# Down projection of a ConvFFN: sample products in six visits, raw weight tiles in a ring of nine, first operands of the second group formed early

## The chip, the core and the metric

The kernel runs on one core of a Trainium2 chip. The metric is the device time of one execution in microseconds, taken as the median of several runs. The engines are PE (TensorE, matrix products; PEld is its weight load), DVE (VectorE), ACT (ScalarE), POOL (GpSimd) and SP (SyncE, which here only issues DMAs). Each engine works through its own instructions in a fixed order. Arrays are fp32; data lies in SBUF with 128 partitions, and PE writes into eight banks of PSUM.

## The reference

One inference step of a one-layer streaming encoder: a token mixer, then a feed-forward part, for 1024 prompt tokens and 32 sample tokens. Only the feed-forward part's last product matters here:

```python
def conv_ffn(xn, buf, w_up, conv_w, conv_b, w_down):
    up = xn @ w_up
    up, buf = causal_dwconv(up, buf, conv_w, conv_b)
    gate, val = jnp.split(up, 2, axis=-1)
    return (jax.nn.gelu(gate, approximate=True) * val) @ w_down, buf
...
x = x + rms_norm(h, g_ffn_post[l])
```

`h = gelu(gate) * val` has 2816 channels, `w_down` is 2816 x 1024.

## The kernel before, in words

The up projection computes h for the prompt in 22 tiles of 128 channels x 1024 tokens (`up_finish`), which go to the DRAM array `h_d`, one DMA each on SP's queue. For the 32 sample tokens it leaves h in SBUF, as `smp_h`.

The down projection (`down_all`) computes the prompt's product with seven products of quarter size, after Strassen: P2, P1, P4, P6, P5, P7, P3, in that order. Each (`run`) loops over p = 0..10 (`NP` = 11), and in each p over four blocks of 128 tokens. An fp32 product is made of three: each operand is split into a high half (a cast on ACT, line 94) and a low half (a subtraction on DVE, line 97), and `mm3` multiplies high by high, high by low and low by high (lines 88, 89, 90). So one p is 12 products of 128 x 512. The operands of step p of product P1 are called P1h (from the tile `ht`, loaded from `h_d`) and P1w (from a raw weight tile, named `wrP` in the profile). ht0 to ht10 belong to P1, ht11 to ht21 to P2. I write "P2 4" for the raw weight tile that P2's p = 4 takes; P2 uses weights 11 to 21, P1 uses 0 to 10, and the other products use sums of weights that were made earlier in DRAM (`ws_d`).

The split operands lie in rings: four tiles for h ("hop"), seven for weights ("op"). The raw weight tiles lie in a ring of six: two in the pool `praw[0]`, four in `ph`. A raw tile of P2 and P1 is read twice: by the split, and by the sample tokens' product.

That product is `sample_products`: the 32 sample tokens times the same raw weights, in plain fp32, for all 22 weight tiles. Four small products, of two weight tiles with two halves each, run side by side in four column groups of PE, 32 columns wide. The profile records two passes for each product (L1618, tile `s`). They are done in visits, after p = 1, 3, 5, 7, 9 and 10 of P2 (into the bank s1) and of P1 (into s2). A raw tile is free for the next load once its visit has read it.

At the end of P2, ACT copies s1 to `keep` (line 1710) and P2's four banks W to `ca` (line 1712). P1 goes into four banks x (`X`), which take the slots of the ring "xw"; s1 takes one of these slots too. Then DVE adds s2 to `keep` and the banks X to `ca`, and P4 begins.

The order of instructions on each engine is set by a planner, which runs a model of the times over the program, with the program's order as priority. `tc.issue_after(ins)` binds it: the instructions of the block stand behind `ins` on ins's engine. Waits on data and on free tiles are added by the planner. `down_raw` loads a raw tile, `load_h` a tile of h; both issue on SP, and in `load_h` the issue stands behind the last raw load (`behind["SP"]`). `rows_of` holds what is done beside each p of P2 (k = 1) and P1 (k = 0): visits and loads. P2's first loads come from `freed`, ahead of the up projection's end (`EARLY` = 3). The row `gp` (the gain of the last norm, broadcast to 128 partitions) is loaded at the start of `down_all`, and ACT turns the sign of half of it.

Of the kernel before, what the change touches and what calls it, by code (L numbers as in the profile page):

```python
# [8 lines left out]
F32 = mybir.dt.float32  # L9
# [3 lines left out]
AF = mybir.ActivationFunctionType  # L13
ALU = mybir.AluOpType
# [4 lines left out]
SEQ = 1024  # L19
# [3 lines left out]
NF = DFF // 128  # L23
# [55 lines left out]
def body(ctx: ExitStack, tc: tile.TileContext, a: dict):  # L79
    nc = tc.nc  # L80
    act, dve, pool, pe, sp = nc.scalar, nc.vector, nc.gpsimd, nc.tensor, nc.sync
# [5 lines left out]
    def mm3(ps, lh, rh, first, last, **kw):  # L87
        pe.matmul(ps, lh[0], rh[0], start=first, stop=False, **kw)  # L88
        pe.matmul(ps, lh[0], rh[1], start=False, stop=False, **kw)  # L89
        return pe.matmul(ps, lh[1], rh[0], start=False, stop=last, **kw)  # L90

    def split(hi, lo, src, eng=None, heng=None):
        if heng is None:
            act.copy(hi, src)
        else:
            heng.tensor_copy(hi, src)
        (eng or pool).tensor_tensor(lo, src, hi.bitcast(F32), op=ALU.subtract)  # L97

    def tanh(out, in_, scale):
        return act.activation(out, in_, AF.Tanh, scale=scale)  # L100
# [4 lines left out]
    psb = ctx.enter_context(tc.tile_pool(name="psb", bufs=3, space=PSUM, reuse_waits="tile"))  # L105
# [19 lines left out]
    h_d = dr.tile([NF, 128, SEQ], F32, name="h_d")  # L125
# [115 lines left out]
    cols_of, dcs_of, behind = {}, {}, {}  # L241
# [969 lines left out]
    upper, jks, kept, pgs = [], [], {}, ExitStack()  # L1211
# [205 lines left out]
    def up_finish(py, f, uu):  # L1417

        ys = []
        for i, j in enumerate((f, NF + f)):  # L1420
            u = uu[i][:, 2:]
            y = py.tile([128, SEQ], F32, tag="y", name=f"y{j}", bufs=3)
            behind["POOL"] = pool.tensor_copy(fhalo[:, j, :], u[:, SEQ - 2:SEQ])  # L1423
            act.activation(y, u, AF.Identity, scale=fconv[:, j, 2:3], bias=fconv[:, j, 3:4])  # L1424
            for s in range(2):
                dve.scalar_tensor_tensor(y, uu[i][:, s:s + SEQ], fconv[:, j, s:s + 1], y, op0=ALU.mult, op1=ALU.add)  # L1426
            ys.append(y)
        act.activation(ys[0], ys[0], AF.Gelu_apprx_tanh)
        kept["gated"] = dve.tensor_tensor(ys[0], ys[0], ys[1], op=ALU.mult)
        sp.dma_start(h_d[f], ys[0])  # L1430

    def up_samples():

# [106 lines left out]
    praw, ph, EARLY = [], [], 3  # L1540

    NP = NF // 2
# [19 lines left out]
            sorted((2 * i + 3 * t, t, i) for i in range((NP + 1) // 2) for t in range(8))]  # L1562

    wraws = {}

    def down_raw(kind, p):

        key = (kind, p if kind in ("P1", "P2") else p // 2)
        if key in wraws:
            return  # L1570
        own = len(wraws) % 6 < 2
        r = (praw[0] if own else ph[0]).tile([128, 2, 512], F32, tag="raw", name=f"wr{kind}_{p}", bufs=2 if own else 4)
        if kind in ("P1", "P2"):
            f = p + NP * (kind == "P2")
            behind["SP"] = sp.dma_start(r.rearrange("p j n -> p (j n)"), a["w_dn"][f])
        else:
            n = min(2, NP - p)
            src = a["w_dn"][NP + p:NP + p + n, :, 512:].rearrange("f p n -> p f n") if kind == "P3" else \
                ws_d[{"P5": 0, "P7": 1, "P6": 2, "P4": 3}[kind]][:, p:p + n, :]
            behind["SP"] = sp.dma_start(r[:, :n, :], src)  # L1580
        wraws[key] = r

    hts = {}

    def load_h(pool_, f):
        hts[f] = pool_.tile([128, SEQ], F32, name=f"ht{f}")
        with tc.issue_after(behind["SP"].ins):
            sp.dma_start(hts[f], h_d[f])

    def ablk(i, k, p):  # L1590
        h = hts[p + NP * k]
        return h[:, 512 * i:512 * i + 512]

    ASRC = dict(P1=(0, 0), P2=(0, 1), P4=(1, 1), P6=(0, 0), P5=(1, 1), P7=(1, 0), P3=(0, 1))

    def halves_of(src, name, pool_, tag, bufs):
        t = pool_.tile([128, 2, 512], F32R, tag=tag, name=name, bufs=bufs)
        split(t[:, 0], t[:, 1], src, dve)
        return t[:, 0], t[:, 1]

    def down_operands(ph, kind, p, early=False):
        down_raw(kind, p)
        h = halves_of(ablk(*ASRC[kind], p), f"{kind}h{p}", ph, "hop", 4)
        wp = (ph, "hop", 4) if early else (praw[1], "op", 7)
        if kind in ("P1", "P2"):
            r = wraws[kind, p]
            w = halves_of(r[:, 0], f"{kind}w{p}", *wp)
        else:
            w = halves_of(wraws[kind, p // 2][:, p % 2], f"{kind}w{p}", *wp)
        return h, w  # L1610

    def sample_products(ps, k, p):

        with tc.issue_after(behind["PE"].ins):
            for q in range(p - p % 2, p + 1):
                for j in range(2):
                    r = 64 * (q % 2) + DEC * j
                    pe.matmul(ps[r:r + DEC], smp_h[:, q + NP * k, :], wraws["P2" if k else "P1", q][:, j],  # L1618
                              start=q < 2, stop=q >= NP - 2)

    def down_all(ph, pc, begun, late):

        CA = pc.tile([128, 4, 2, 512], F32, name="ca")
        CB = pc.tile([128, 4, 2, 512], F32, name="cb")
        gp = pc.tile([128, 1024], F32, name="gp")
        sp.dma_start(gp, a["grows"][1:2, :].broadcast_to([128, 1024]))
        act.activation(gp[:, 512:], gp[:, 512:], AF.Copy, scale=-1.0)
        ssp = late.enter_context(tc.tile_pool(name="p11", bufs=1, side="right", reuse_waits="tile"))

        def w_banks(name):  # L1630
            return [psf.tile([128, 512], F32, tag="sx", name=f"{name}0", bufs=1)] + \
                [psb.tile([128, 512], F32, tag="big", name=f"{name}{i}", bufs=3) for i in range(1, 4)]

        def run(kind, banks, first, last, each=None, n_end=0):
            end = []
            for p in range(NP):
                ops = begun.pop((kind, p), None) or down_operands(ph, kind, p)
                if p >= NP - n_end:
                    end.append((p, ops))
                    continue  # L1640
                h, w = ops
                for i in range(4):
                    c = slice(128 * i, 128 * i + 128)
                    behind["PE"] = mm3(banks[i], (h[0][:, c], h[1][:, c]), w, first and p == 0, last and p == NP - 1,
                                       skip_group_check=True)
                if each:
                    each(p, w)
            return end
# [41 lines left out]
        def scratch(u):  # L1690
            return pc.tile([128, 4], F32, tag="fss", name=f"gss{u}", bufs=9)

        def rows_of(k, bank):

            def each(p, w):
                if p % 2 or p == NP - 1:
                    sample_products(bank, k, p)
                if k:
                    for f in (NP + EARLY + p, p - NP + 6):
                        if 0 <= f < NF and f not in hts:  # L1700
                            load_h(ph if f >= NP else ssp, f)
                elif p + 6 < NP:
                    load_h(ssp, p + 6)
            return each

        s1 = psf.tile([128, 512], F32, tag="xw", name="s1", bufs=4)
        W = w_banks("q2")
        run("P2", W, True, True, rows_of(1, s1))
        keep = pc.tile([128, 512], F32, name="keep")
        act.copy(keep, s1)  # L1710
        for i in range(4):
            act.copy(CA[:, i, 0], W[i])

        X = [psf.tile([128, 512], F32, tag="xw", name=f"x{i}", bufs=4) for i in range(4)]
        s2 = psb.tile([128, 512], F32, tag="big", name="s2", bufs=3)
        run("P1", X, True, False, rows_of(0, s2))
        dve.tensor_tensor(keep, keep, s2, op=ALU.add)
        quarter = pc.tile([DEC, 3, 512], F32, name="quarter")
        for b in range(3):
            sp.dma_start(quarter[:, b], keep[DEC * (b + 1):DEC * (b + 2)])  # L1720
# [3 lines left out]
        W = w_banks("q4")  # L1724
# [9 lines left out]
        W = w_banks("q5")  # L1734
# [35 lines left out]
        W = w_banks("q3")  # L1770
# [10 lines left out]
        def each(p, w):  # L1781
            if p < 4:
                upper_half(p)
# [76 lines left out]
    p4s, p5s, p6s, p7s, p8s, p9s, pxs, phs, late = (ExitStack() for _ in range(9))  # L1860
# [3 lines left out]
    psf = p4s.enter_context(tc.tile_pool(name="psf", bufs=1, space=PSUM, reuse_waits="tile"))  # L1864
# [5 lines left out]
    own = {"c1": pt.tile([128, 256], F32, name="c1_00")}  # L1870
# [7 lines left out]
    X = col_operands(px, q0, 0, parts="B")  # L1878
# [49 lines left out]
    begun = {}  # L1928

    def freed():  # L1930
        pxs.close()
        ph.append(phs.enter_context(tc.tile_pool(name="ph", bufs=1, side="left", reuse_waits="tile")))
        for p in range(EARLY):
            down_raw("P2", p)
            load_h(ph[0], NP + p)
        down_raw("P2", EARLY)
# [166 lines left out]
```

## Time and profile before

| what | value |
|---|---|
| median of 3 runs | 1350.47 us (1350.0 to 1354.46) |
| the profiled execution | 1351.36 us, its span 1349.6 us |
| granted TensorE clock, mean | 0.988 |
| PE busy | 1301.8 us (96%) |
| DVE, ACT, POOL busy | 1009.9, 700.2, 281.7 us |
| P2's first product to P1's last | 1110.5 to 1189.2 us |
| L1618, 88 passes | 1120.8 to 1190.2 us |
| P4 and P6 | 1190.1 to 1250.2 us |

A line of the order in time gives the start in us from the span's start, the length, the engine, the line of the kernel, the operation, out<-in, the shape and the number of merged instructions; in brackets stands the idle time of the engine ahead of it and what ended it. The chain of work gives start, length, engine, tile and line. A line on one tile's instructions gives the shortest, median and longest in ns, and when the first and the last start.

### The profile page before, as it was taken

Reading aid. Unit: us, or ns where it says so; the run is one execution under the profiler, and the core shown is the slowest. Engines: PE = TensorE matmul, PEld = TensorE weight load, DVE = VectorE, ACT = ScalarE, POOL = GpSimd, SP = SyncE. Lnnn points to the kernel's source line nnn. Section 1 sums busy time; section 2 is a strip of 40 time slices with the busy share of each in tenths; the row PEclk is TensorE's granted clock in tenths of the full one; section 3 lists DMA queues with packets and bytes.
Section 4 is the critical chain, followed back from the end, with each engine's and each line's share of the span. In section 5 each row is a group of like instructions: output and inputs, shape, how many; then the busy total and the mean of one; then the engine's idle time right before and its main releaser. Section 6 shows DMA issues by size and latency. Waiting matters only on the chain.

```text
span 1349.6 us, 25577 instructions
## 1 busy us (share of the span) xinstructions
PE 1301.8 (96%) x9896; PEld 1097.7 (81%) x9896; DVE 1009.9 (75%) x1761; ACT 700.2 (52%) x1298; POOL 281.7 (21%) x399
## 2 busy tenths in 40 slices
PE   6999999998999999999999999999999999999997
PEld 6999899998888987767877777778888886678885
DVE  5795649778698778876898676778888875499566
ACT  5555556555575555535754444444555454454552
POOL 4531403136022254313100010110111000010005
PEclk9999999999998999989999999999999999999998
DMA  8699878886789964543627988864674349644435
GB/s 339 233 350 362 279 245 256 281 282 219 270 254 313 326 200 134 183 146 104 192 82 237 312 225 282 217 185 134 155 168 137 99 158 356 254 162 141 144 106 124
DMA packets 134784, 291.73 MB, mean 216 GB/s; under 512 B 29015, under 2 KB 63991, under 8 KB 132535
## 3 DMA queue, kind: packets, MB, share of 16 engines
q1 hardware_dynamic: 121031, 267.03, 58.4%
q0 software_dynamic: 9120, 18.62, 7.8%
q10 hardware_dynamic: 4512, 4.46, 1.0%
q8 instruction: 77, 1.26, 0.4%
q14 instruction: 44, 0.36, 0.1%
HBM read 229.38 MB, written 85.78 MB: 234 GB/s over the span
## 4 chain that ended last, share of the span: by engine, by line
PE 64%; DVE 8%; ACT 2%; issue 1%; POOL 1%; DMA 1%; DVEq 0%; POOLq 0%; SPq 0%; ACTq 0%
PE pux_None L88 4%; PE pux_None L89 4%; PE pux_None L90 4%; PE q L88 3%; PE puw_None L88 3%; PE puw_None L89 3%; PE puw_None L90 3%; PE q L89 3%; PE q L90 3%; PE x L88 2%; PE x L89 2%; PE x L90 2%; PE zp L90 2%; PE zp L88 2%; PE zp L89 2%; PE us L1457 2%
## 5 line engine op out<-in xcount | busy, mean ns | idle before, releaser
L1426 DVE SCALAR_TENSOR_TENSOR y<-uu,fconv_sb,y 128x1024 f32<-128x1024 f32 x88 | 112.8, 1282 | 22.9 <-ACT y L1424 21.8
L1423 POOL COPY fhalo<-uu 128x2 f32<-128x2 f32 x44 | 17.1, 388 | 388.8 <-DVE uu L1341 388.8
L88 PE MATMUL pv<-wt_0h,xh 128*128 128x256 f32 (+1 forms) x192 | 55.9, 291 | 5.5 <-DVE xl L321 1.6
L90 PE MATMUL zp<-woh,cl 128*128 128x512 f32 (+1 forms) x144 | 57.3, 398 | 1.4 <-DVE cl L1093 1.4
L1424 ACT ACTIVATE y<-uu,fconv_sb 128x1024 f32<-128x1024 f32 x44 | 54.8, 1245 | 6.8 <-DVE uu L1341 5.9
L88 PE MATMUL zp<-woh,ch 128*128 128x512 f32 (+1 forms) x144 | 56.9, 405 | 1.0 <-ACT ch L1092 0.8
L89 PE MATMUL zp<-wol,ch 128*128 128x512 f32 (+1 forms) x144 | 57.4, 399 | 0.3 <-DVE wol L97 0.3
L90 PE MATMUL pv<-wt_1h,xl 128*128 128x256 f32 (+1 forms) x192 | 54.9, 286 | 0.0
L88 PE MATMUL pv<-wt_1h,xh 128*128 128x256 f32 (+1 forms) x192 | 54.5, 284 | 0.0
L90 PE MATMUL pv<-wt_0h,xl 128*128 128x256 f32 (+1 forms) x192 | 54.4, 283 | 0.0
L89 PE MATMUL pv<-wt_0l,xh 128*128 128x256 f32 (+1 forms) x192 | 54.2, 282 | 0.0
L89 PE MATMUL pv<-wt_1l,xh 128*128 128x256 f32 (+1 forms) x192 | 54.2, 282 | 0.0
L1673 POOL TENSOR_TENSOR gss<-gss 128x1 f32<-128x1 f32 (+1 forms) x9 | 8.6, 952 | 185.1 <-ACT gjk L1666 185.1
L208 POOL TENSOR_SCALAR hrs<-hss 128x5 f32<-128x5 f32 (+3 forms) x27 | 10.1, 376 | 174.5 <-DVE hss L1002 171.9
L88 PEld LDWEIGHTS pv<-wt_0h,xh 128*128 128x128 f32 x192 | 35.9, 187 | 7.6 <-DVE xl L321 2.2
L818 DVE COPY_PREDICATED P<-masks_sb,sc 128x352 f32<-128x352 int32 (+3 forms) x53 | 37.8, 713 | 5.0 <-PE sc L731 4.4
L209 POOL TENSOR_TENSOR hrs<-hrs,mhalf 128x5 f32<-128x5 f32 (+3 forms) x27 | 37.2, 1376 | 2.2
L88 PEld LDWEIGHTS pv<-wt_1h,xh 128*128 128x128 f32 x192 | 35.9, 187 | 0.7 <-issue 0.6
L1002 DVE TENSOR_REDUCE hss<-sq 128x5 f32<-128x320 f32 (+3 forms) x27 | 13.6, 502 | 30.4 <-ACT sq L1001 30.4
L90 PEld LDWEIGHTS pv<-wt_1h,xl 128*128 128x128 f32 x192 | 35.9, 187 | 0.3
L90 PEld LDWEIGHTS pv<-wt_0h,xl 128*128 128x128 f32 x192 | 35.9, 187 | 0.2
L89 PEld LDWEIGHTS pv<-wt_0l,xh 128*128 128x128 f32 x192 | 35.9, 187 | 0.1
(1898 smaller groups left out, 4652.3 us busy)
## 6 DMA issues: line engine op xcount, KB each, us to landing
wus<-in_w_us SPq DMA_DIRECT2D x16, 1024.0 KB, 6.3
wrP<-in_w_dn SPq DMA_DIRECT2D x27, 512.0 KB, 3.9
h_d<-y SPq DMA_DIRECT2D x22, 512.0 KB, 4.4
ht<-h_d SPq DMA_DIRECT2D x22, 512.0 KB, 7.1
wt_0r<-in_w_tok SPq DMA_DIRECT2D x21, 512.0 KB, 5.6
wt_1r<-in_w_tok SPq DMA_DIRECT2D x21, 512.0 KB, 6.6
ws_d<-in_w_dn POOLq DMA_DIRECT2D x20, 512.0 KB, 6.6
wrP<-ws_d SPq DMA_DIRECT2D x20, 512.0 KB, 3.9
```

The lines of the kernel that those rows point to most:

```text
L88: pe.matmul(ps, lh[0], rh[0], start=first, stop=False, **kw)
L89: pe.matmul(ps, lh[0], rh[1], start=False, stop=False, **kw)
L90: return pe.matmul(ps, lh[1], rh[0], start=False, stop=last, **kw)
L208: pool.tensor_scalar(out, ss, 1.0 / width, eps, op0=ALU.mult, op1=ALU.add)
L209: pool.tensor_tensor(out, out, mhalf[:n, :cols], op=ALU.pow)
L818: dve.copy_predicated(dst, mk.broadcast_to([n, 11, *mk.shape[2:]]), src)
L1002: dve.tensor_reduce(ss[:n, h0:h0 + nh], sq3, axis=mybir.AxisListType.X, op=ALU.add)
L1423: behind["POOL"] = pool.tensor_copy(fhalo[:, j, :], u[:, SEQ - 2:SEQ])
L1424: act.activation(y, u, AF.Identity, scale=fconv[:, j, 2:3], bias=fconv[:, j, 3:4])
L1426: dve.scalar_tensor_tensor(y, uu[i][:, s:s + SEQ], fconv[:, j, s:s + 1], y, op0=ALU.mult, op1=ALU.add)
L1457: pe.matmul(ps[DEC * q:DEC * q + DEC], smp_x[:, k, :], ring[i % 3][:, q, :], start=k == 0, stop=k == 7)
L1673: pool.tensor_tensor(ss[:n, 0:1], ss[:n, 2:3], ss[:n, 3:4], op=ALU.add)
```

## The change

- `sample_products` takes a list of weight tiles, and is called after p = 3 (tiles 0 to 3), p = 7 (4 to 7) and p = 9 (8 to 10, with the raw tile of p = 10 asked for first) of P2 and of P1: six visits in all. The bank s2 is taken at the first visit of P1, s1 at that of P2.
- The ring of raw tiles has nine slots for P2 and P1: two in `praw[0]`, five in `ph`, two in `ssp`, the pool of ht0 to ht10; seven for the later products. Their loads are bound to stand in order.
- `load_h` now counts as the last load on SP, so that the next one stands behind it. P2's loads of raw tiles 4 to 10 and of ht17 to ht20 are asked for after p = 3, then P1's raw tiles 0 and 1 and ht21. P1's raw tiles 2 and 3 follow at p = 7, then ht0; ht1 and ht2 at p = 8, ht3 and ht4 at p = 9, and ht5 at p = 10. `gp` is loaded after p = 9, and its sign turned at P1's p = 1.
- P1's operands of p = 0 and 1 are formed at the end of P2. In P1, the cast of each h stands on ACT behind the cast of the weights before it. `keep` stands behind the cast of P1's second h, and the copies to `ca` behind `keep`, asked for at P1's p = 1.
- The last store to `h_d` is issued by POOL.

The core of the diff:

```diff
-        sp.dma_start(h_d[f], ys[0])
+        (pool if f == NF - 1 else sp).dma_start(h_d[f], ys[0])
...
+    VISITS_D = {3: range(4), 7: range(4, 8), NP - 2: range(8, NP)}
...
-        own = len(wraws) % 6 < 2
-        r = (praw[0] if own else ph[0]).tile([128, 2, 512], F32, tag="raw", name=f"wr{kind}_{p}", bufs=2 if own else 4)
+        n = len(wraws) % (9 if kind in ("P1", "P2") else 7)
+        pool_, bufs = (praw[0], 2) if n < 2 else (ph[0], 5) if n < 7 else (praw[2], 2)
+        r = pool_.tile([128, 2, 512], F32, tag="raw", name=f"wr{kind}_{p}", bufs=bufs)
...
-            behind["SP"] = sp.dma_start(r.rearrange("p j n -> p (j n)"), a["w_dn"][f])
+            with ExitStack() as order:
+                if wraws:
+                    order.enter_context(tc.issue_after(behind["raw"].ins))
+                behind["raw"] = behind["SP"] = sp.dma_start(r.rearrange("p j n -> p (j n)"), a["w_dn"][f])
...
+        if f not in hts:
+            place_h(pool_, f)
         with tc.issue_after(behind["SP"].ins):
-            sp.dma_start(hts[f], h_d[f])
+            behind["SP"] = sp.dma_start(hts[f], h_d[f])
...
-        h = halves_of(ablk(*ASRC[kind], p), f"{kind}h{p}", ph, "hop", 4)
+        late = tc.issue_after(kept["w"].ins) if kind == "P1" and p else ExitStack()
+        with late:
+            h = halves_of(ablk(*ASRC[kind], p), f"{kind}h{p}", ph, "hop", 4)
+            kept["h"] = kept["w"]
...
-                if p % 2 or p == NP - 1:
-                    sample_products(bank, k, p)
+                if p == 1:
+                    first()
+                if p in VISITS_D:
+                    if p == NP - 2:
+                        down_raw("P2" if k else "P1", p + 1)
+                    banks.append(banks[0] if banks else bank())
+                    sample_products(banks[0], k, VISITS_D[p])
+                if k and p == 3:
+                    for q in range(p + 1, NP):
+                        down_raw("P2", q)
+                        if q < 8:
+                            load_h(ph, NP + EARLY - 1 + q)
                 if k:
-                    for f in (NP + EARLY + p, p - NP + 6):
-                        if 0 <= f < NF and f not in hts:
-                            load_h(ph if f >= NP else ssp, f)
-                elif p + 6 < NP:
-                    load_h(ssp, p + 6)
+                    if p < 3:
+                        load_h(ph, NP + EARLY + p)
+                    if p == 3:
+                        for q in range(2):
+                            down_raw("P1", q)
+                        load_h(ph, NF - 1)
+                    if p == 7:
+                        for q in range(2, 4):
+                            down_raw("P1", q)
+                    if p == NP - 1:
+                        for q in range(2):
+                            begun["P1", q] = down_operands(ph, "P1", q)
+                    for f in {7: (0,), 8: (1, 2), 9: (3, 4), 10: (5,)}.get(p, ()):
+                        load_h(ssp, f)
+                else:
+                    if p + 4 < NP:
+                        down_raw("P1", p + 4)
+                    if p + 6 < NP:
+                        load_h(ssp, p + 6)
...
+        def leave_q2():
+            with tc.issue_after(kept["keep"].ins):
+                for i in range(4):
+                    act.copy(CA[:, i, 0], W[i])
...
-        act.copy(keep, s1)
-        for i in range(4):
-            act.copy(CA[:, i, 0], W[i])
+        with tc.issue_after(kept["h"].ins):
+            kept["keep"] = act.copy(keep, srow[0])
...
-        run("P1", X, True, False, rows_of(0, s2))
-        dve.tensor_tensor(keep, keep, s2, op=ALU.add)
+        run("P1", X, True, False, rows_of(0, lambda: sample_bank(psb, "big", "s2", 3), leave_q2))
+        dve.tensor_tensor(keep, keep, srow[1], op=ALU.add)
```

More of the change, by code (lines that the diff above doesn't have):

```diff
@@ L92, in split @@
     def split(hi, lo, src, eng=None, heng=None):
[L93 to L96, printed above, removed]
+        ins = act.copy(hi, src) if heng is None else heng.tensor_copy(hi, src)
         (eng or pool).tensor_tensor(lo, src, hi.bitcast(F32), op=ALU.subtract)
+        return ins
     def tanh(out, in_, scale):
@@ L1583, in body, with place_h @@
     hts = {}
+    def place_h(pool_, f):
+        hts[f] = pool_.tile([128, SEQ], F32, name=f"ht{f}")
+    loaded = set()
     def load_h(pool_, f):
-        hts[f] = pool_.tile([128, SEQ], F32, name=f"ht{f}")
+        if f in loaded:
+            return
+        loaded.add(f)
+        if f not in hts:
+            place_h(pool_, f)
         with tc.issue_after(behind["SP"].ins):
-            sp.dma_start(hts[f], h_d[f])
+            behind["SP"] = sp.dma_start(hts[f], h_d[f])
     def ablk(i, k, p):
@@ L1597, in halves_of @@
         t = pool_.tile([128, 2, 512], F32R, tag=tag, name=name, bufs=bufs)
-        split(t[:, 0], t[:, 1], src, dve)
+        kept["w"] = split(t[:, 0], t[:, 1], src, dve)
         return t[:, 0], t[:, 1]
@@ L1610, in down_operands, with sample_products @@
         return h, w
-    def sample_products(ps, k, p):
+    def sample_products(ps, k, qs):
         with tc.issue_after(behind["PE"].ins):
-            for q in range(p - p % 2, p + 1):
+            for q in qs:
                 for j in range(2):
@@ L1625, in down_all @@
         gp = pc.tile([128, 1024], F32, name="gp")
-        sp.dma_start(gp, a["grows"][1:2, :].broadcast_to([128, 1024]))
-        act.activation(gp[:, 512:], gp[:, 512:], AF.Copy, scale=-1.0)
         ssp = late.enter_context(tc.tile_pool(name="p11", bufs=1, side="right", reuse_waits="tile"))
+        praw.append(ssp)
+        for f in range(4):
+            place_h(ssp, f)
         def w_banks(name):
@@ L1691, in scratch, with rows_of @@
             return pc.tile([128, 4], F32, tag="fss", name=f"gss{u}", bufs=9)
-        def rows_of(k, bank):
+        def rows_of(k, bank, first=lambda: None):
+            banks = []
             def each(p, w):
-                if p % 2 or p == NP - 1:
-                    sample_products(bank, k, p)
-                if k:
-                    for f in (NP + EARLY + p, p - NP + 6):
-                        if 0 <= f < NF and f not in hts:
-                            load_h(ph if f >= NP else ssp, f)
-                elif p + 6 < NP:
-                    load_h(ssp, p + 6)
-            return each
@@ L1706, in down_all @@
-        s1 = psf.tile([128, 512], F32, tag="xw", name="s1", bufs=4)
+                if p == 1:
[10 more added lines that the diff above has]
+                            load_h(ph, NP + EARLY - 1 + q)
@@ new lines, in each, with sample_bank @@
+                if k and p == 9:
+                    with tc.issue_after(behind["SP"].ins):
+                        sp.dma_start(gp, a["grows"][1:2, :].broadcast_to([128, 1024]))
+                if not k and p == 1:
+                    act.activation(gp[:, 512:], gp[:, 512:], AF.Copy, scale=-1.0)
+            return each
+        def sample_bank(pool_, tag, name, bufs):
+            srow.append(pool_.tile([128, 512], F32, tag=tag, name=name, bufs=bufs))
+            return srow[-1]
+        def leave_q2():
+            with tc.issue_after(kept["keep"].ins):
+                for i in range(4):
+                    act.copy(CA[:, i, 0], W[i])
@@ L1707, in down_all @@
+        srow = []
         W = w_banks("q2")
-        run("P2", W, True, True, rows_of(1, s1))
+        run("P2", W, True, True, rows_of(1, lambda: sample_bank(psf, "xw", "s1", 4)))
         keep = pc.tile([128, 512], F32, name="keep")
-        act.copy(keep, s1)
-        for i in range(4):
-            act.copy(CA[:, i, 0], W[i])
+        with tc.issue_after(kept["h"].ins):
+            kept["keep"] = act.copy(keep, srow[0])
         X = [psf.tile([128, 512], F32, tag="xw", name=f"x{i}", bufs=4) for i in range(4)]
-        s2 = psb.tile([128, 512], F32, tag="big", name="s2", bufs=3)
```

## The prediction, made before the changed kernel ran

> **What bounds the kernel now.** I read the page's busy times first, then the stretches of the down projection, then the chain of work, then each engine in order of time around the two places that the diff touches.
>
> ```profile
> PE 1301.8 (96%) x9896; PEld 1097.7 (81%) x9896; DVE 1009.9 (75%) x1761; ACT 700.2 (52%) x1298; POOL 281.7 (21%) x399
> 1121.00:1150.00 29.00, 29.00 (x143) 19.59 (x136) 14.72 (x22) 10.78 (x19) 0.00 (x0) 1.00 0.97 346
> 1150.00:1156.00 6.00, 4.13 (x16) 1.90 (x15) 1.71 (x3) 4.71 (x9) 0.00 (x0) 1.00 1.03 420
> 1156.00:1190.00 34.00, 34.00 (x164) 22.56 (x162) 20.01 (x33) 13.50 (x25) 0.00 (x0) 1.00 0.62 220
> 1220.00:1240.00 20.00, 20.00 (x90) 16.57 (x89) 20.00 (x35) 10.99 (x22) 1.63 (x2) 1.00 0.41 112
> ```
>
> The columns of a stretch are its length, then busy time of PE, PEld, DVE, ACT, POOL, the granted clock, DMA share and GB/s. TensorE bounds the kernel, and in the groups P2 and P1 (1110 to 1190 us) it is busy throughout except for 1.87 us in 1150 to 1156, where P2 hands over to P1. So the change can win there by taking PE work out or by closing that gap, and nowhere else in these 80 us. The last row warns: in P6 DVE is as full as PE.
>
> **The six visits.** Before, `sample_products` runs after p = 1, 3, 5, 7, 9, 10 of each group, 12 visits; after, after p = 3, 7, 9, 6 visits. The products are the same.
>
> ```profile
> 1138.84 1.00 PE s L1618 x8
> 1145.51 1.00 PE s L1618 x8
> 1158.56 1.00 PE s L1618 x8
> 1189.18 0.98 PE s L1618 x4
> 1203.08 0.91 PE q L90 x4
> 1205.80 0.91 PE q L90 x4
> 1132.11 1.06 PE L1618 MATMUL s<-wrP,smp_h 128*32 128x512 f32 x8
> L1618 PE MATMUL s<-wrP,smp_h x88: 592/605/617, 1120.8 to 1189.6; 128*32 128x512 f32 x88
> ```
>
> Without visits a p of 12 products takes 1205.80 - 1203.08 = 2.72 us, 0.227 each. From visit to visit there are 1145.51 - 1138.84 = 6.67 us, and 24 products are 5.44, so a visit costs 1.23. Its eight passes go four at a time, in two rounds: first start to last end 1.06, one pass 0.605, so a round takes 0.455 and two take 0.91. The other 0.32 is entry and exit. The visit with four passes takes 0.98, as long as one with eight, so rounds are paid, not passes. Rounds stay at 12 per group (4 + 4 + 4 for 2 x 6, since p = 10 alone also takes two). Six entries go: 6 x 0.32 = 1.9 us. Bounds: 0, if the 0.32 goes with each pair of rounds, to 1.9. A loss is excluded as no pass is added. I take 1.9, because the four-pass row says that the extra does not follow the amount of work in a visit.
>
> The Trainium skill, "TensorEngine Tiling (Array Packing)", Key Properties, says that changing the tiling mode drains the TensorE, while tiles within one mode run independently. The visits change from 128 to 32 columns and back, so by it 12 of 24 changes go. By the contrary reading, a cost of each 32-column round, nothing would go and the sum would be 2.4 in place of 4.3. The rows agree with the drain as far as one visit shows; no row has four rounds in a visit.
>
> **The hand-over from P2 to P1.**
>
> ```profile
> 1151.73 0.96 PE L90 MATMUL x<-P1w,P1h 128*128 128x512 f32 x3
> 1153.34 0.50 PE L88 MATMUL x<-P1w,P1h 128*128 128x512 f32 x1 [0.64 <-ACT keep L1710]
> 1155.53 1.20 PE L88 MATMUL x<-P1w,P1h 128*128 128x512 f32 x4 [1.23 <-ACT P1w L94]
> 1150.23 2.05 ACT L1712 COPY ca<-q 128x512 f32<-128x512 f32 x4 [4.03 <-PE q L90]
> 1152.14 0.65 ACT L94 CAST P1h<-ht 128x512 fp32r<-128x512 f32 x1
> 1152.66 0.62 ACT L1710 COPY keep<-s 128x512 f32<-128x512 f32 x1
> 1154.34 0.62 ACT L94 CAST P1h<-ht 128x512 fp32r<-128x512 f32 x1 [1.05 <-PE x L90]
> 1154.86 1.14 ACT L94 CAST P1w<-wrP 128x512 fp32r<-128x512 f32 x2
> ```
>
> ACT had stood idle 4.03 us before the four `ca` copies. `keep` frees the bank of the fourth x product and waits behind them, and the weights of P1's p = 1 wait behind an h cast that itself waits for PE. Price: 1158.56 - 1145.51 = 13.05 us between two visits, less two visits (2.46) and 36 products (12 of P2, 24 of P1: 8.16), leaves 2.43. After the change both operands of p = 0 and 1 are formed ahead, `keep` follows P1h1's cast, the last P2 visit stands at p = 9, one p (2.72 us) before the end, and the `ca` copies (2.05 on ACT) come at p = 1, needed by nobody before s2's bank at p = 3. I take the whole 2.43; bounds 0 to 2.43, and below zero only through late tiles.
>
> **Tiles on SP's queue.** This is where a cost can come in. SP issues in order; load_h is now chained behind the last load of either kind.
>
> ```profile
> 1125.54 1.22 DVE L1429 TENSOR_TENSOR y<-y,y 128x1024 f32<-128x1024 f32 x1
> 1127.43 0.38 SPq L1430 DMA_DIRECT2D h_d<-y  x1
> 1127.87 0.42 SPq L1626 DMA_DIRECT2D gp<-in_grows  x1
> 1135.89 5.25 SPq L1588 DMA_DIRECT2D ht<-h_d  x8
> 1137.10 0.63 ACT L1627 ACTIVATE gp<-gp 128x512 f32<-128x512 f32 x1 [1.91 <-DMA gp<-in_grows]
> 1144.02 0.62 ACT L94 CAST P2h<-ht 128x512 fp32r<-128x512 f32 x1 [3.11 <-DMA ht<-h_d]
> DMA to landing us min/median/max: 3.5/3.9/10.0
> L1559 POOL DMA_DIRECT2D ws_d<-in_w_dn x24: 855/1145/1814, 732.9 to 1044.3; - x24
> DMA to landing us min/median/max: 4.3/6.6/9.9
> ```
>
> The first landing row is that of the raw tiles (wrP), the second that of POOL's transfers to ws_d. Before, the last gated tile is ready at 1126.76; its store is issued at 1127.43, ht21 is issued 8.5 us later, once the store has landed, and P2h10 is cast 3.11 us late, though still ahead of PE. POOL issues the store after: it costs POOL 0.9 to 1.8 us (idle there) and lands 4.3 to 9.9 us after issue, so 1131 to 1137, and ht21 is no later than now. Nine raw slots let P2 4 to 8 start without a visit's release; P2 9 and 10 and P1 0 and 1 wait for the visit at p = 3. PE reaches it one visit earlier than now, 1125.51 - 1.23 = 1124.3, and leaves it at 1126.4.
>
> New is a wait: P1 2 and 3 take the slots of P2 4 and 5, freed inside the visit at p = 7 (1126.4 + 4 x 2.72 = 1137.3, tiles free about 1138.4), and ht0 to ht5 and gp are queued behind them. At 420 GB/s (stretch 1150 to 1156) 512 KB take 1.25 us. P1 2 lands about 1138.4 + 3.9 = 1142.3, or 1143 with the issues between, P1 3 1144.3, ht0 1145.5, ht1 1146.8. PE leaves P2 at 1137.3 + 2.1 + 5.44 + 2.1 + 2.72 = 1149.7. P1h0 needs ht0 plus cast and subtraction (0.62 + 0.69): 1146.8, ready 2.9 us ahead; P1h1 1148.1, needed 1152.4; `keep` after its cast, 1148. So it fits, with 2.9 us of cover; every us that ht0 is later than that costs one.
>
> gp's load moves from 1127.87 to about 1142 and its scaling on ACT (0.63) to P1's p = 1. With the 9.2 us that it took above it lands at 1151; the casts queued behind it on ACT are those of p = 2 and 3, due at PE from 1155.1. I count 0, and 2 to 3 us at the worst, which the far end of the range holds. Its first reader on DVE comes only with P1's sums, after 1185.
>
> Further on, P1's raw tile 4 is tenth in this row: 1138.4 + 2.6 + 10 x 1.25 = 1153.5, plus some 2 to 3 us if gp (9.2 us from issue to landing above) slows the row; needed 1149.7 + 4 x 2.72 + 2.1 - 1.3 = 1161.4. Cover 5 us. Rows and needs then run at the same pace, two tiles in 2.5 us against 2.72.
>
> **The stages behind.**
>
> ```profile
> 1173.41 17.11 SPq L1580 DMA_DIRECT2D wrP<-ws_d  x9
> 1184.44 1.29 DVE L97 TENSOR_TENSOR P4w<-wrP,P4w 128x512 fp32r<-128x512 f32 x2 [1.13 <-ACT P4w L94]
> 1201.89 0.67 DVE L97 TENSOR_TENSOR P4h<-ht,P4h 128x512 fp32r<-128x512 f32 x1
> 1202.92 0.84 PE L90 MATMUL q<-P4w,P4h 128*128 128x512 f32 x3
> 1229.00 0.67 DVE L97 TENSOR_TENSOR P6h<-ht,P6h 128x512 fp32r<-128x512 f32 x1
> 1230.12 1.07 PE L90 MATMUL x<-P6w,P6h 128*128 128x512 f32 x4
> ```
>
> In P4 and P6 DVE's low halves come 1202.92 - 1202.56 = 0.36 and 1230.12 - 1229.67 = 0.45 us before PE takes them. When PE is 4.3 us early, DVE must be as much earlier. Its work there starts from h slots that PE frees and from P1's end, which both move along. P4's first raw pair does not: its slot comes free in P1's visit at p = 7 (1149.7 + 8 x 2.72 + 2.1 + 2.1 = 1175.7), not at 1173.41, landing about 1179.5 with P4 due at 1185.7. Against that, P1's last operands are split earlier. I count 0 here; bounds 0 to 2.8 (two P4 weights, 1.29, and the idle 1.13 again, with 0.4 over).
>
> **Sum.** 1.9 + 2.43 = 4.3 off the profiled 1351.36 (span 1349.6): 1347.0. The median, 1350.47, stands 0.89 below that run, so 1346.2.
>
> **Rivals.**
> A. DVE keeps P4 and P6: PE comes early and waits there. For it: the two slacks above. Against: most of DVE's releases are PE's own. It gives back 1 to 2.8: 1347.2 to 1349.0.
> B. The hand-over does not close: `keep` or P1w1 still stands behind something on ACT, in an order that the scheduler sets and the diff only partly binds. Visits alone: 1350.47 - 1.9 = 1348.6; or half the gap left, 1347.4.
> C. The other side: ht0 and what is queued with it come late, because SP stands at P1 2's slot and the scheduler puts P2's second visit late. With those products done only at p = 9, the slot is free at 1146.9, 8.5 us later; ht0 then lands at 1154.0, where 1148.4 (1145.5 and the cover of 2.9) is the latest without a stall, so PE stands 5.6 us: 1346.2 + 5.6 = 1351.8. The change turns into a loss when ht0 lands after 1152.7 (4.3 of stall) and into one past 0.3% after 1157 (8.4), which takes gp's slow row ahead of it as well: 1354.5. For it: SP cannot pass a waiting load. Against: the release is PE's own, PE is never idle there now, and DMA has room, 346 GB/s in 1121 to 1150 beside 420.
>
> The Trainium skill, "SBUF — State Buffer", The DVE blocks DMA trap (SWDGE), says that a DMA issued from POOL can wait for its descriptors while DVE holds a shared port in a two-port copy. No such copy of DVE stands in the rows here, so it adds no term. If it did, the store would be late and ht21 with it, which is rival C's wait by another road.
>
> **How the numbers follow.** Full gain 0.55, A 0.18, B 0.14, C and other new waits 0.13. About 0.3% (4.05 us) is what a measurement of this kernel can tell from no change, and the full gain, 4.3, lies only just past it: of its 0.55 I put 0.43 past the line and 0.12 inside. So faster 0.43, same 0.12 + 0.18 + 0.14 = 0.44, slower 0.13. The likeliest case's own range is 1345.2 to 1347.2. The range for 8 in 10 runs from 1345.0 through A and B to 1352.0, C's nearer end, which leaves out C's far part and little below.
>
> **What would show it.** Six groups of L1618, the long ones about 2.1 us with 16 passes (1.9 right), or 2.4 (wrong); no idle PE row between the last q of P2 and the fourth x of P1, `keep` before all `ca` copies; h_d's last store on POOL with ht21 cast earlier than 1144; ht0 landed by 1147 and no PE idle before 1190 minus 4.3. A stall with DVE P4h or P6h as releaser means A; ACT keep or P1w, B; DMA ht or wrP, C. Wrong altogether would be any PE idle of over 1 us elsewhere in the down projection.

## The result, and the profile after

In interleaved runs of both kernels, the kernel before took 1352.84 us in the median (1347.34 to 1358.39, 22 runs) and the changed one 1346.92 us (1338.8 to 1353.73, 22 runs): a ratio of 0.9957, 95% interval 0.9942 to 0.9972. The predicted time was 1346.2, the predicted gain 4.3 us (0.32%); the interval of the ratio is 3.8 to 7.8 us. The profiled execution took 1350.5 us, its span 1348.7. One run of the changed kernel, among the twelve of its repeat below, took 2124.86 us at a granted clock of 0.556; it is in no ratio.

Single runs of one kernel differ by up to 15 us, so the trace needs a yardstick that leaves this out. Up to P2 both kernels have the same instructions in the same order on each engine. I take the first product of the last up block, from the order in time on PE, first of before and then of after:

```profile
1092.84 0.39 PE L88 MATMUL puw_None<-T1h,S_21h 128*128 128x512 f32 x1
```

```profile
1096.42 0.39 PE L88 MATMUL puw_None<-T1h,S_21h 128*128 128x512 f32 x1
```

From this product to the end of the span (all of the down projection and the tail) I write D. Worked out from the unrounded records it is 256.71 us before and 252.30 after: **4.41 us less**. The changed kernel came to this point 3.6 us later in its profiled run; that is why the two spans differ by 0.8 only. In the twelve profiles of this study the point lies between 1090.3 and 1097.3 us, in no order that follows the edits, while D repeats: 252.30 and 252.32 in two profiles of the changed kernel whose spans are 1348.7 and 1342.9.

The stretches of after, with the columns of before's (length, then PE, PEld, DVE, ACT, POOL, clock, DMA share, GB/s):

```profile
1121.00:1150.00 29.00, 29.00 (x147) 19.94 (x145) 17.26 (x25) 12.65 (x22) 0.80 (x2) 1.00 0.88 339
1150.00:1156.00 6.00, 6.00 (x27) 4.81 (x26) 1.85 (x4) 4.20 (x8) 0.00 (x0) 1.00 1.02 410
1220.00:1240.00 20.00, 20.00 (x90) 16.57 (x89) 20.00 (x35) 11.35 (x20) 0.00 (x0) 1.00 0.36 108
```

PE's 1.87 us of idle time in 1150 to 1156 are gone, and no new idle time stands on PE from the last up block to P3. DVE is still full in P6. The visits and the hand-over, in order of time on PE:

```profile
1127.79 1.93 PE L1633 MATMUL s<-wrP,smp_h 128*32 128x512 f32 x16
1140.79 1.92 PE L1633 MATMUL s<-wrP,smp_h 128*32 128x512 f32 x16
1148.35 1.91 PE L1633 MATMUL s<-wrP,smp_h 128*32 128x512 f32 x12
...
1152.17 1.08 PE L90 MATMUL q<-P2w,P2h 128*128 128x512 f32 x4
1153.08 0.39 PE L88 MATMUL x<-P1w,P1h 128*128 128x512 f32 x1
...
1164.06 1.92 PE L1633 MATMUL s<-wrP,smp_h 128*32 128x512 f32 x16
```

From the first visit to the second, 13.00 us hold 48 products (10.88 at 0.2267) and one visit, which costs 2.12; two short visits cost 2.46. So some 0.33 us go with each visit taken away. From 1148.35 to 1164.06, over the hand-over, 15.71 us hold 60 products (13.60) and a visit (2.11): nothing is left. The work that stood in the way on ACT, same kernel, in order of time:

```profile
1145.47 0.62 ACT L93 CAST P1w<-wrP 128x512 fp32r<-128x512 f32 x1 [2.91 <-DMA wrP<-in_w_dn]
...
1149.06 0.62 ACT L93 CAST P1h<-ht 128x512 fp32r<-128x512 f32 x1 [1.69 <-DMA ht<-h_d]
1150.37 0.62 ACT L93 CAST P1h<-ht 128x512 fp32r<-128x512 f32 x1 [0.69 <-DMA ht<-h_d]
1150.89 0.58 ACT L1767 COPY keep<-s 128x512 f32<-128x512 f32 x1
1152.65 2.06 ACT L1760 COPY ca<-q 128x512 f32<-128x512 f32 x4 [1.17 <-PE q L90]
1154.56 1.17 ACT L93 CAST P1h<-ht 128x512 fp32r<-128x512 f32 x2
```

Both h casts of P1's first two steps and `keep` now stand ahead of the `ca` copies, and the copies run beside P1. The new wait is there, on data: ACT stands 1.69 us for ht0.

### The profile page after: what moved, and what is told of

Same layout as the page of the kernel before. It is cut to its first block, busy times and chain, and to the rows that moved or that the text cites. A ratio compares the mean times of both kernels' runs of the same rounds, so it can differ in the third digit from the quotient of the medians.

```text
span 1348.7 us, 25587 instructions
## 1 busy us (share of the span) xinstructions
PE 1301.8 (97%) x9896; PEld 1100.0 (82%) x9896; DVE 1011.0 (75%) x1761; ACT 700.6 (52%) x1298; POOL 284.0 (21%) x400
## 4 chain that ended last, share of the span: by engine, by line
PE 63%; DVE 9%; ACT 2%; issue 1%; POOL 1%; DMA 1%; DVEq 0%; POOLq 0%; ACTq 0%; SPq 0%
PE pux_None L88 4%; PE pux_None L90 4%; PE pux_None L89 4%; PE puw_None L88 3%; PE puw_None L90 3%; PE puw_None L89 3%; PE q L88 3%; PE q L90 3%; PE q L89 3%; PE x L88 2%; PE x L89 2%; PE x L90 2%; PE zp L88 2%; PE zp L90 2%; PE zp L89 2%; PE us L1455 2%
```

## The experiments

All D are from one profile each; the repeat above shows what that is worth (0.02 us). Changed lines are shown against the changed kernel, except where it says otherwise. First the changed kernel once more:

> The changed kernel once more, unchanged. The yardstick for all runs is the distance D from the first product of the last up block that is in T1 (puw from T1h, S_21h) to the end of the span: 256.7 us in the kernel before, 252.3 in the changed one. If D is set by the program alone, it comes out within 0.3 of 252.3, whatever the start of the stretch is; the whole time may differ by some us, because the stretch begins at another moment. Rival: D itself varies by the microseconds by which whole runs vary, and then a profile tells nothing of 4 us.

Measured: D 252.32; median 1348.39 us (12 runs), ratio 0.9971, interval 0.9956 to 0.9985. It agrees with the first ratio and, with 2.0 to 6.0 us, holds the trace's 4.4.

**Is it the visit that costs?** Ten visits in place of six:

```diff
-    VISITS_D = {3: range(4), 7: range(4, 8), NP - 2: range(8, NP)}
+    VISITS_D = {1: range(2), 3: range(2, 4), 5: range(4, 6), 7: range(6, 8), NP - 2: range(8, NP)}
```

> Ten visits (p = 1, 3, 5, 7, 9 in each group) in place of six, all else as changed. By the theory that a visit has an entry price of 0.32 us and that rounds are otherwise equal: D = 252.3 + 4 x 0.32 = 253.6. By the rival that the extra goes with the rounds, which stay 12 per group: 252.3. The hand-over stays without idle time in both.

Measured: D 253.64, 1.34 more for four more visits, with no idle time of PE: 0.33 each. The visit, not the round, carries the extra.

**Fewer still.** Two visits per group:

```diff
-    VISITS_D = {3: range(4), 7: range(4, 8), NP - 2: range(8, NP)}
+    VISITS_D = {3: range(4), NP - 2: range(4, NP)}
```

> Four visits in all: p = 3 (tiles 0 to 3) and p = 9 (4 to 10). Two entries fewer: -0.64. But P1's raw tiles 2 and 3 now take slots that come free only in P2's visit at p = 9, some 4.6 us later than with the visit at p = 7, and ht0 stands behind them on SP. By the theory (2.9 us of cover, then one for one) PE stands still some 1.5 us at the hand-over: D = 252.3 - 0.6 + 1.5 = 253.2, with ACT P1h as the releaser. By the rival that the tiles of h are early enough anyway: 251.7.

Measured: D 254.15, 0.95 more than I expected. At the hand-over PE stands for ht0, whose issue waits behind P1's raw tiles 2 and 3, which wait for P2's late visit (rival C's wait). PE in order of time, at the hand-over and at P4's start:

```profile
1152.60 0.50 PE L88 MATMUL x<-P1w,P1h 128*128 128x512 f32 x1 [1.35 <-ACT P1h L93]
...
1190.25 0.50 PE L89 MATMUL q<-P4w,P4h 128*128 128x512 f32 x1 [0.27 <-DVE P4w L94]
```

Product by product against the changed kernel, the first wait costs 1.57 us, as expected. The miss is the second one, which I had not foreseen: PE falls 0.86 us further behind at P4's start.

**The same with the h tiles first.** If that were all, asking for ht0 to ht5 ahead of the two raw tiles would mend it:

```diff
+    VISITS_D = {3: range(4), NP - 2: range(4, NP)}
...
-                    if p == 7:
-                        for q in range(2, 4):
-                            down_raw("P1", q)
                     for f in {7: (0,), 8: (1, 2), 9: (3, 4), 10: (5,)}.get(p, ()):
                         load_h(ssp, f)
+                    if p == 9:
+                        for q in range(2, 4):
+                            down_raw("P1", q)
```

> As the run with four visits, but ht0 to ht5 are asked for ahead of P1's raw tiles 2 and 3, so they do not wait for the visit at p = 9. By the theory the stall is gone and the two entries remain: D = 252.3 - 0.64 = 251.7. If the hand-over still stalls, the cause is not the place in SP's queue but the release of the slots itself.

Measured: D 253.06; median 1348.35 (12 runs), ratio 0.9974, interval 0.9958 to 0.999. The stall at the hand-over is gone, but the wait at P4's start is still there and larger: it costs 1.16 us. ACT, then PE, of this kernel in order of time:

```profile
1188.12 3.22 ACT L93 CAST P4w<-wrP 128x512 fp32r<-128x512 f32 x6 [5.28 <-DMA wrP<-ws_d]
```

```profile
1190.52 0.50 PE L89 MATMUL q<-P4w,P4h 128*128 128x512 f32 x1 [0.51 <-DVE P4w L94]
```

P4's first raw pair takes a slot that P1's last visit frees. That visit, with seven tiles, now ends at 1185.7; the pair is issued within it, at 1184.1, and lands at 1188.1, when the cast begins. In the changed kernel it is issued at 1179.0, as the visit at p = 7 ends, and lands at 1183.0. The next three runs take parts of the change away, one by one.

**The last store back on SP.**

```diff
-        (pool if f == NF - 1 else sp).dma_start(h_d[f], ys[0])
+        sp.dma_start(h_d[f], ys[0])
```

> As changed, but the last store to h_d goes on SP's queue as before. The theory counts this edit at nothing: D = 252.3, since P2h10 has over 7 us to spare in the changed kernel. Rival: the store is what brings ht21, and behind it ht0, in time; on SP's queue it stands behind the waits for raw slots, ht21 and ht0 come 1 to 4 us later and D rises by up to 1 us.

Measured: D 252.26. The store's queue is worth nothing, either way.

**Without the operands formed ahead.**

```diff
-                    if p == NP - 1:
-                        for q in range(2):
-                            begun["P1", q] = down_operands(ph, "P1", q)
```

> As changed, but P1's first two operands are not formed at the end of P2; loads, visits, keep and the copies are asked for as changed. On ACT one of the copies to ca then stands ahead of P1h0, and it waits for P2's end. By the theory PE waits for that copy and for the cast, about 0.6 + 0.6: D = 252.3 + 1.2 = 253.5. Rival (the early loads and the last visit at p = 9 are what closes the gap): 252.3. Rival (forming ahead is all of it): 252.3 + 2.4 = 254.7.

Measured: D 253.52, 1.2 more as expected, but only 0.83 of it at the hand-over. ACT in order of time, then PE, and last DVE and PE in P6:

```profile
1147.96 0.59 ACT L1757 COPY ca<-q 128x512 f32<-128x512 f32 x1 [1.23 <-PE q L90]
1148.45 0.62 ACT L93 CAST P1h<-ht 128x512 fp32r<-128x512 f32 x1
1148.96 1.56 ACT L1757 COPY ca<-q 128x512 f32<-128x512 f32 x3
```

```profile
1149.12 0.50 PE L88 MATMUL x<-P1w,P1h 128*128 128x512 f32 x1 [0.56 <-ACT P1h L93]
```

```profile
1227.62 0.67 DVE L94 TENSOR_TENSOR P6h<-ht,P6h 128x512 fp32r<-128x512 f32 x1
1228.35 1.19 PE L90 MATMUL x<-P6w,P6h 128*128 128x512 f32 x4
```

One copy stands ahead of P1's first h cast, and P1 starts late: 0.56 us of idle time, 0.83 us in all. Another 0.33 us are lost in P6, where the planner put this low half one DVE instruction later and PE now takes it 0.06 us after it is ready. So the number was hit partly by luck, and forming ahead is worth 0.83 of the 2.43 us at the hand-over. The other 1.6 come with what this run keeps (an early `keep`, the last visit at p = 9, the order of the loads); no run takes these apart.

**The kernel before, with six visits and nothing else.** `VISITS_D` and the list of tiles go into the kernel before; its ring of six, its loads and its hand-over stay:

```diff
-                if p % 2 or p == NP - 1:
-                    sample_products(bank, k, p)
+                if p in VISITS_D:
+                    if p == NP - 2:
+                        down_raw("P2" if k else "P1", p + 1)
+                    sample_products(bank, k, VISITS_D[p])
```

> The kernel before with the six visits alone: ring of six raw tiles, loads and hand-over as before. By the sum's first term alone D = 256.7 - 1.9 = 254.8. By the theory that the ring of nine is what makes long visits free: P1's first raw tile now waits for the visit at p = 7 and is cast behind the four copies to ca, so the hand-over costs 3.5 to 5 us in place of 2.4, and P2's raw tile 6 comes just in time or 1 to 2 us late: D between 256 and 258.

Measured: D 257.96, 1.25 *more* than before. PE, then SP, in order of time:

```profile
1148.72 1.06 PE L1619 MATMUL s<-wrP,smp_h 128*32 128x512 f32 x8
1152.87 1.05 PE L1619 MATMUL s<-wrP,smp_h 128*32 128x512 f32 x4 [3.08 <-DMA wrP<-in_w_dn]
...
1158.74 1.19 PE L88 MATMUL x<-P1w,P1h 128*128 128x512 f32 x4 [1.85 <-ACT P1w L94]
```

```profile
1140.81 3.12 SPq L1589 DMA_DIRECT2D ht<-h_d  x5
1144.04 0.74 SPq L1576 DMA_DIRECT2D wrP<-in_w_dn  x1
```

With six slots, P2's last raw tile takes that of P2 4, which no visit reads before the one after p = 7 (it starts at 1141.16). SP issues it at 1144.04, behind five tiles of h; it lands 8.8 us later, at 1152.8, and PE stands 3.08 us for it. P2's last visit splits in two, so five entries are saved: 256.71 - 5 x 0.33 + 3.08 = 258.1. D lies in the range that I gave, but by another wait than I named: the hand-over did not grow to 3.5 to 5 us (its idle time is 1.85 us in one wait, in place of 1.87 in two), and P2's raw tile 10 was late, not 6. The first term is payable only where this tile comes in time. The changed kernel gives it a free slot and a place ahead of the later tiles of h; no run here separates the two.

**Is DVE's slack in P4 and P6 real?** Four multiplications of 128x512 that nobody reads, on DVE at P4's second step:

```diff
-            dve.tensor_tensor(a21, a11, a21, op=ALU.subtract)
+            kept["c"] = dve.tensor_tensor(a21, a11, a21, op=ALU.subtract)
+            if p == 1:
+                with tc.issue_after(kept["c"].ins):
+                    for i in range(4):
+                        dve.tensor_tensor(CB[:, i, 1], gp[:, :512], gp[:, 512:], op=ALU.mult)
```

> As changed, with four idle multiplications of 128x512 on DVE (0.60 us each, into a tile that is overwritten later) behind P4's second combination. The changed kernel leaves DVE's low halves 0.46 us ahead of PE at the least, in P6. By the theory that DVE is the next bound there, 2.4 - 0.46 = 1.9 us come out as PE idle time in P4 and P6: D = 254.2. Rival: the order of work lets DVE catch up (its idle time at P5 begins at 1246): D = 252.3.

Measured: D 254.82, 2.5 more. DVE, then PE in P6, in order of time:

```profile
1179.56 2.49 DVE L1674 TENSOR_TENSOR cb<-gp 128x512 f32<-128x512 f32 x4
```

```profile
1220.68 0.39 PE L89 MATMUL x<-P6w,P6h 128*128 128x512 f32 x1
1221.24 1.21 PE L90 MATMUL x<-P6w,P6h 128*128 128x512 f32 x4 [0.17 <-DVE P6h L94]
...
1223.90 0.39 PE L89 MATMUL x<-P6w,P6h 128*128 128x512 f32 x1
1225.45 1.20 PE L90 MATMUL x<-P6w,P6h 128*128 128x512 f32 x4 [1.16 <-DVE P6h L94]
```

About 2.5 us reach the end: 0.5 at P4's start, where PE waits for P4w's low half, and nearly 2.0 some 40 us later, as waits for P6h. I had expected 1.9 of idle time; 1.44 us are idle time, 0.11 of them at P4's start, and each of the three stops costs some 0.3 us more (see the last section). The planner also orders DVE's work a little differently here (the low half that PE waits for at 1225.45 is 3.1 us later than in the changed kernel, not 2.5), so the run does not tell what P6's slack of 0.46 us swallowed. It does show that DVE is the next bound behind PE in P4 to P6.

**Two versions that take up what these runs showed.** First, P2 in two visits with its h tiles first, and P1 in three, so that P4's slots come free as early as in the changed kernel:

```diff
-    VISITS_D = {3: range(4), 7: range(4, 8), NP - 2: range(8, NP)}
+    VISITS_D = [{3: range(4), 7: range(4, 8), NP - 2: range(8, NP)},
+                {3: range(4), NP - 2: range(4, NP)}]
```

> P2 in two visits (0 to 3, then 4 to 10), its tiles of h asked for ahead of P1's raw tiles 2 and 3, P1 in three visits as in the changed kernel. Theory (a visit costs one entry of 0.33 us, and the wait at P4's start came from P1's long last visit, which held the raw slots): one visit less and no new wait, D = 252.3 - 0.33 = 252.0 us, and no wait on a raw tile at P4's start. Rival (the wait at P4's start came from the moved loads of P2's end): D about 253.0, as with two visits in both groups.

Then P1 in two as well, split at p = 5, and P4's first raw tiles in the slots that this visit frees:

```diff
+    VISITS_D = [{5: range(6), NP - 2: range(6, NP)},
+                {3: range(4), NP - 2: range(4, NP)}]
...
-        n = len(wraws) % (9 if kind in ("P1", "P2") else 7)
+        n = len(wraws) % 9 if kind in ("P1", "P2") else (len(wraws) + 1) % 7
```

> As the run before it, and P1 in two visits after p = 5 (0 to 5) and p = 9 (6 to 10), with P4's first raw tiles taking the slots that the first of these visits frees. Four visits in all. Theory: D = 252.3 - 2 x 0.33 = 251.65 us, no wait at P4's start. Rival (any long last visit of P1 costs P4's first tiles their time): D 252.5 to 253.1, with DVE or ACT of P4's weights as the releaser.

Measured: D 252.13 and 251.75, both without a wait of PE. Up to P3's last products they are 0.45 and 0.82 us ahead of the changed kernel; 0.27 of that is lost in the tail, for which no run gives a cause. At P4's start the leads were 0.45 and 0.91, more than the 0.33 for each visit; P6 gave 0.09 of the second back, its smallest slack on DVE being 0.08 us there. So the wait in the two-visit kernel came from P1's long last visit, not from the moved loads. The second one on ACT at P4's start, in order of time:

```profile
1177.95 0.62 ACT L93 CAST P4h<-ht 128x512 fp32r<-128x512 f32 x1 [1.58 <-PE x L90]
1178.48 2.18 ACT L93 CAST P4w<-wrP 128x512 fp32r<-128x512 f32 x4
```

Where the two-visit kernel had 5.28 us of waiting for the load, P4's weights are cast here with none, some 7.6 us before PE needs them (1186.1). Medians: 1347.06 (10 runs; ratio 0.9961, interval 0.9938 to 0.9984) and 1347.5 (10 runs; 0.9954, 0.993 to 0.9979). Both beat the kernel before; a lead of 0.2 to 0.55 us over the changed kernel shows in D alone, the runs cannot tell it.

## Why the prediction was right, point by point

- **Six visits, 1.9 us.** Right: 6 x 0.33 = 2.0, a little past the bound of 1.9. A four-round visit shows 1.92 us and costs 2.12, where the rows of one visit had given 2.1 (right) against 2.4 (wrong). By the drain of the Trainium skill, "TensorEngine Tiling (Array Packing)", Key Properties, the extra goes with the change of mode; the ten-visit kernel agrees, with 0.33 for each visit put back. No run tells a drain from another cost that comes once with each visit.
- **The hand-over, 2.43 us.** Right: nothing is left of it, and `keep` stands before the `ca` copies. Product by product, PE is 3.41 us ahead of before when P1 is under way (three visits and the hand-over), and 1.0 more when P4 is (three visits). The two terms add up to 4.43; the trace gives 4.41. Forming ahead is shown to carry 0.83 of the 2.43; the rest is not divided.
- **The price of the first term alone.** Here a rival's working failed: "visits alone 1348.6" left out the ring. In the old ring, with the old loads, the visits alone cost 1.25 us. So "a loss is excluded" holds for the work on PE only, not for the tiles that a longer visit holds back. The term stood in the sum because the ring of nine and its order of loads came with it.
- **ht0, 2.9 us of cover.** Right within 0.5. SP and POOL after, first in order of time on SP, then the answer on the store and ht21 (1129 to 1142 us):

```profile
1138.59 0.33 SPq L1600 DMA_DIRECT2D ht<-h_d  x1
1141.88 0.80 SPq L1578 DMA_DIRECT2D wrP<-in_w_dn  x2
1142.74 2.46 SPq L1600 DMA_DIRECT2D ht<-h_d  x5
1145.24 0.56 SPq L1748 DMA_DIRECT2D gp<-in_grows  x1
```

```profile
L1428 POOL DMA_DIRECT2D h_d<-y x1: 610/610/610, 1130.6 to 1130.6; - x1
DMA to landing us min/median/max: 3.3/5.6/7.9
```

  This run is 3.6 us late, so ht0's issue at 1142.74 is 1139.2 by before's clock. P1's raw tile 2 went out within the visit at p = 7, as said. It landed when its cast began, at 1149.0, by before's clock 1145.4, where 1145.5 was predicted. PE took the high half 3.4 us after it was ready, the low half 4.0. The two-visit kernel shows what that cover is worth: there it is used up, and PE stands.
- **The store on POOL, nothing.** Right in the price and in the times, but for the issue, which took POOL 0.61 us where 0.9 to 1.8 were counted. It landed 7.9 us after its issue at 1130.64, at 1138.6, which is 1135.0 by before's clock and inside 1131 to 1137; ht21's issue followed at once. P2h10 was cast at 1141.95, 7.6 us before PE took it, against 1.8 before. But with the store on SP D is the same, so the gain in slack bought nothing.
- **P4 and P6 on DVE, nothing.** Right, and close: the low halves of h in P6 lie 0.46 us or more ahead of PE (0.45 before), those in P4 2.5 or more (0.36 before). After, DVE and PE at the two closest places:

```profile
1209.76 0.67 DVE L94 TENSOR_TENSOR P4h<-ht,P4h 128x512 fp32r<-128x512 f32 x1
1212.92 1.07 PE L90 MATMUL q<-P4w,P4h 128*128 128x512 f32 x4
...
1230.83 0.67 DVE L94 TENSOR_TENSOR P6h<-ht,P6h 128x512 fp32r<-128x512 f32 x1
1231.96 1.07 PE L90 MATMUL x<-P6w,P6h 128*128 128x512 f32 x4
```

  DVE moved along with PE, as the step said, and P4's first raw pair landed at 1183.0, by before's clock 1179.5, as predicted. The four multiplications show rival A's mechanism: work added to DVE there comes out at the end.
- **The size of the ratio.** 0.9957 is 5.8 us, the trace's D 4.4. The interval holds both, and the repeat's ratio of 0.9971 (3.9 us) lies on the other side of 4.4. Nothing in the trace asks for more than 4.4. That the median came within 0.7 us of the predicted 1346.2 is partly luck: the prediction started from 1350.47, the median of three runs of before, which over 22 runs became 1352.84, and the gain of the medians, 5.9 us, is 1.5 larger than the trace's. The prediction gave the full gain 0.55, and called it only just past the 0.3% that can be told from no change; the two ratios lie on either side of that line.

## What to carry to other kernels

A short burst in another tile shape costs an entry and an exit (here 0.33 to 0.45 us) besides its rounds, so fewer and longer bursts win, if every buffer that the burst frees has another slot to stand in: price the load that waits for the longer burst, at both ends of the stage, before counting the entries. At a hand-over between two accumulation groups, look at the order on the engine that drains the banks: what the next group needs first (its operands, the one bank it lacks) goes ahead of the copies that nobody waits for. And where whole runs scatter more than the effect, measure from a fixed instruction behind the scatter.

## What the runs showed of the hardware that was not expected

- **A stop of PE costs more than its idle time.** In the kernel with the extra multiplications, the product at 1223.90 and the next at 1225.45 are 1.55 us apart where 0.227 is normal: 1.32 lost, and 1.16 recorded as idle. The four products that follow take 1.20 where four elsewhere take 1.08. So about 0.3 us come on top of the idle time, and as much at the stop of 0.17 (0.56 between the products, then 1.21). The hand-over before shows the same: 1.87 us of idle time in two stops cost 2.43. In the kernel without operands formed ahead, the product at 1228.35 shows no idle time at all, and with the three behind it still loses 0.28 us.
- **An operation of 32 x 1 elements on POOL took 6 us beside a full DVE.** After, on POOL and then on DVE, in order of time:

```profile
1200.17 6.08 POOL L1689 TENSOR_TENSOR gss<-gss 32x1 f32<-32x1 f32 x1 [68.93 <-ACT gjk L1682]
```

```profile
1205.53 0.67 DVE L94 TENSOR_TENSOR P4h<-ht,P4h 128x512 fp32r<-128x512 f32 x1
1207.22 0.74 DVE L1696 SCALAR_TENSOR_TENSOR keep<-keep,gss,gp 32x512 f32<-32x512 f32 x1 [1.02 <-POOL gss L207]
```

  On 128 x 1 elements the same line takes 0.19 to 1.52 us later in this profile. It ends at 1206.25, 0.05 us after DVE's last subtraction (1206.20), when DVE itself stops to wait for what POOL makes of it; before, it ends 0.06 us after DVE stops. In all twelve profiles it ends so, whether it took 4.8 or 7.0 us. The Trainium skill, "SBUF — State Buffer", Who interferes with whom, says that a DVE instruction with two SBUF inputs contends with a GpSimd instruction that reads SBUF, and that the order of issue decides which of the two is blocked. The rows agree that the two contend; here POOL stayed blocked through a whole row of DVE instructions, and no experiment took DVE's work away from it. DVE loses 1.0 us there, in both kernels, in the stages where it is the next bound.
- **Where the scatter of single runs arises.** It lies ahead of the down projection, 7 us between profiles of nearly the same instructions, and it goes with the granted clock. Of the changed kernel's 22 runs the fastest (1338.8 us) had a mean of 0.993 and the slowest (1353.73) one of 0.985; over all 22 the correlation of time and clock is -0.86. In its two profiles the clock is 0.97 and 0.98 in the mean from 100 to 700 us, the higher one in the profile that is 5.8 us shorter, and 1.00 in both from 700 to 1336 us. So D, up to the tail, lies where the clock was full, which is why it repeats. What lowers the clock stays open, and whether it is all of the scatter.
